# Splitting the normalised rows in the front part and re-ordering the dense part's buffers in a hybrid decoder step

## The chip, the cores and the metric

The kernel runs on one core of a Trainium2 chip. The metric is device time in microseconds (us) of the whole program, the median of several executions. One further execution was recorded by the hardware profiler; its span (first to last instruction) and its own time are given below.

## The reference

One inference step of a one-layer decoder with float32 data: a prompt of 1024 tokens (8 tiles of 128 rows) and a decode batch of 32 tokens (8 sequences of 4, called the sample tile). What matters here is the order of the computation:

```python
h = rms(x) * (1 + sc1) + sh1;  proj = h @ w_in
mix = concat(dilated_attention(proj), rwkv7(proj)) @ w_out
x = x + g1 * mix
h2 = rms(x) * (1 + sc2) + sh2            # the normalised rows of this case
x = x + g2 * peer(h2)                    # 8 heads x top-16 of 128*128 single-neuron experts
```

`peer` scores the 16384 experts by two sums of keys, takes 16 for each head, and adds `gate * gelu(h2 . u) * v` of the chosen ones.

## The kernel before

**Two ways through the experts.** For the prompt tiles 0 to 4 (`dense_set`, 640 rows) the experts are computed densely: all 16384 hidden values of a row by matmul, multiplied by a matrix of gates that is zero where an expert was not chosen, and multiplied by all of `expert_v`. For tiles 5, 6, 7 and the sample tile the 128 chosen rows of `expert_u` and `expert_v` are gathered for each token by indirect DMA.

**Precision.** A float32 matmul operand is split into two values of the type fp32r, `hi` and `lo` (`split`, line 230: a cast on ScalarE, then a subtraction on VectorE or GpSimd). `mm3` (line 243) then makes three matmuls: `hi x hi`, `hi x lo`, `lo x hi`.

**Stages in time.** Up to about 640 us: projections and part of RWKV. From 640 us to about 1690 us the *front part* (lines 1789 to 1876): RWKV of the last prompt tiles, attention, and for each tile in turn `project_out` (output projection, second norm, writes `h2A`, feature by row, two buffers), `route_scores` (scores and their best 16), `route_pick` (the 16 experts of each head) and, for tiles 0 to 4, `spread_gates` (the gate matrix, staged in a tile of 16 KB per partition and written to `g_d` in HBM). Then attention of tiles 6 and 7, `rwkv_sample` and `attn_sample`. From about 1700 us to the end the *dense part* (`dense`, line 1615) runs with the gathers and with the routing of tiles 6, 7 and the sample tile between its steps.

**How the rows reach the dense part.** In `front()` (line 1823) each dense tile's `h2A` is written to `h2_f` in HBM as float32 (line 1830, five DMAs, the last at 1248 us). At the start of the dense part (lines 1878 to 1887) `h2_f` is loaded in eight pieces into the tile `dacc`, which is free until the first output is summed there, and each piece is split into `h2T[0]` (hi) and `h2T[1]` (lo): eight casts on ScalarE and eight subtractions on VectorE, 128x640 each.

**The dense loop.** `hidden(b)` (line 1623) loads a block of `u` in two DMAs, splits it into `uh` (ScalarE) and `ul` (GpSimd), and computes for each half of the 640 rows 8 x 3 matmuls against `h2T`; GELU, gate and a split into `ch`, `cl` follow. `values` (line 1649) loads and splits `v` into `vh`, `vl`. `output` (line 1658) sums four blocks into `dacc`. Buffers: `u` three, `uh` and `ul` two each, `vh` and `vl` five each.

**What sets the order.** The parts are Python generators that `weave` (line 276) interleaves by a planner's costs; the framework then orders each engine's instructions by priority and by when their inputs and buffers are expected, and inserts the semaphores. All loads and stores go through SP's queue, in its order; the gathers go through GpSimd's. Each of SP's transfers also waits until the eighth transfer before it has landed.

**Memory.** Pools are stacks in each partition, one growing from the left and one from the right. A tile that is laid over tiles of a closed pool waits, at its first use, for the last use of every tile that it overlaps (`reuse_waits="tile"`), whichever part of it is used first. On the left lie, in bytes of a partition: `spread` 21888 to 48512 (the stage at 32128 to 48512), `tops_A` to 52608, `pick` to 63424, `front` to 88224, attention behind it. The dense pool lies over them from 22912: `dacc` to 43392, `uh` to 51584, `ul` to 59776, `u` to 65920, then `ch`, `cl`, the gates `g`, `v`, `vh`, `vl`. On the right `h2T[0]` takes 188384 to 208864 and `h2T[1]` 208864 to 229344; before them lie there the tiles of `attn_sample`, whose last one, `smo`, is at 222464 to 222976. `smo` is the attention result of the last four sample sequences; it is made from `so`, which is transposed through the one PSUM bank `rs` that `rwkv_sample`'s last transposes (of `yts`) use as well.

All engine instructions are recorded under line 196, that of a helper, so the profile's rows are told apart by the names of their tiles. `h_f` in a row is `h2_f`.

Of the kernel before, what the change touches and what calls it, by code (L numbers as in the profile page):

```python
# [11 lines left out]
FT = mybir.dt.float32  # L12
FR = mybir.dt.float32r
I32 = mybir.dt.int32
# [11 lines left out]
H = 8  # L26
# [175 lines left out]
def tile_hybrid_step(ctx, tc, ins, outs):  # L202
# [6 lines left out]
    def open_pool(es, name, side="left"):  # L209
        return es.enter_context(tc.tile_pool(name=name, bufs=1, side=side, reuse_waits="tile"))  # L210
# [1206 lines left out]
    def route_pick(pick, tops, i, eng=ve):  # L1417

        pa, place = pick
        nh = H if i < NT else 2  # L1420
        v, iu = (x[i][:, :2 * nh] for x in tops)
        eid, gate = (x[i][i][:, :TOPK * nh] for x in (eids, gates))
        fi = pa.tile([128, 16, TOPK], FT, tag="tf", name="tf", bufs=1)[:, :2 * nh]
        ve.tensor_copy(fi, iu)
        v4 = v.rearrange("p (h a) k -> p h a k", a=2)
        f4 = fi.rearrange("p (h a) k -> p h a k", a=2)
        ve.tensor_scalar(f4[:, :, 0], f4[:, :, 0], 128.0, None, op0=OP.mult)
        cand = pa.tile([128, TOPK, NCAND], FT, tag="tq", name="tc", bufs=2)[:, :nh]
        cid = pa.tile([128, H, NCAND], FT, tag="td", name="td", bufs=1)[:, :nh]
        o = 0  # L1430
        for i0, ni, nj in RECTS:
            for x, y in ((cand, v4), (cid, f4)):
                ve.tensor_tensor(x[:, :, o:o + ni * nj].rearrange("p h (i j) -> p h i j", i=ni),
                                 y[:, :, 0, i0:i0 + ni, None].to_broadcast([128, nh, ni, nj]),
                                 y[:, :, 1, None, :nj].to_broadcast([128, nh, ni, nj]), op=OP.add)
            o += ni * nj
        code = cid.bitcast(I32)
        ve.tensor_tensor(code, cid, place[:, None, :].to_broadcast([128, nh, NCAND]), op=OP.add)
        top = pa.tile([128, H, TOPK], FT, tag="tt", name="tt", bufs=1)[:, :nh]
        pu = pa.tile([128, H, TOPK], U32, tag="tp", name="tp", bufs=1)[:, :nh]  # L1440
        r = pa.tile([128, TOPK, NCAND], FT, tag="tq", name="ts", bufs=2)[:, :nh]
        for h in range(nh):
            ve.max(top[:, h, :8], cand[:, h])
        for h in range(nh):
            ve.match_replace(r[:, h], top[:, h, :8], cand[:, h], -3.0e38)
        for h in range(nh):
            ve.max_index(pu[:, h, :8], top[:, h, :8], cand[:, h])
        for h in range(nh):
            ve.max(top[:, h, 8:], r[:, h])
        for h in range(nh):  # L1450
            ve.max_index(pu[:, h, 8:], top[:, h, 8:], r[:, h])
        yield
        pf = pa.tile([128, H, TOPK], I32, tag="te", name="te", bufs=1)[:, :nh]
        ve.tensor_scalar(pf, pu.bitcast(I32), 14, None, op0=OP.logical_shift_left)
        sh = [128, TOPK, NCAND]
        eqs = []
        for h in range(nh + 1):
            if h < nh:

                eq = pa.tile(sh, I32, tag="tq", name="tq", bufs=2)  # L1460
                eqs.append(eq)
                eng.tensor_tensor(eq, code[:, h, None, :].to_broadcast(sh), pf[:, h, :, None].to_broadcast(sh), op=OP.subtract)
            if h:
                ve.tensor_reduce(eid[:, TOPK * (h - 1):TOPK * h], eqs[h - 1].bitcast(U32), axis=AX.X, op=OP.min)
                yield
        gs = pa.tile([128, H], FT, tag="th", name="th", bufs=1)[:, :nh]
        gv = gate.rearrange("p (h k) -> p h k", h=nh)
        ve.tensor_tensor(gv, top, top[:, :, :1].to_broadcast([128, nh, TOPK]), op=OP.subtract)
        sc.activation(gate, gate, AF.Exp)
        ve.tensor_reduce(gs, gv, axis=AX.X, op=OP.add)  # L1470
        ve.reciprocal(gs, gs)
        ve.tensor_tensor(gv, gv, gs[:, :, None].to_broadcast([128, nh, TOPK]), op=OP.mult)
        yield
# [138 lines left out]
        sc.copy(hi, src)  # L1612
        (gp if j in POOL_LO else ve).tensor_tensor(lo, src, hi.bitcast(FT), op=OP.subtract)

    def dense(pa, pp, acc, h2T, tiles):

        nt = len(tiles)
        n = 128 * nt
# [2 lines left out]
        gate2 = {}  # L1621

        def hidden(b):
            uh = pa.tile([128, KD, 128], FR, tag="uh", name="uh", bufs=2)
            ul = pa.tile([128, KD, 128], FR, tag="ul", name="ul", bufs=2)
            for x in range(2):
                ks = slice(4 * x, 4 * x + 4)
                u = pa.tile([128, 4, 128], FT, tag="u", name="u", bufs=3)
                sy.dma_start(u, A["uT"][b, :, ks])
                split2(u, uh[:, ks], ul[:, ks], 8 + b % 2)  # L1630
            ch = pa.tile([128, n], FR, tag="ch", name="ch", bufs=NG + EARLY)
            cl = pa.tile([128, n], FR, tag="cl", name="cl", bufs=NG + EARLY)
            for h in range(2):
                if b % 4 == 0:
                    G_[h] = pa.tile([128, n // 64, 4, 32], FT, tag="g", name="g", bufs=3)
                    sy.dma_start(G_[h], g_d[n // 64 * h:n // 64 * (h + 1), :, b:b + 4].rearrange("s e i t -> e s i t"))
                cs = slice(h * n // 2, (h + 1) * n // 2)
                ps = pp("d")
                for k in range(KD):
                    mm3(ps[:, :n // 2], (uh[:, k], ul[:, k]), [x[:, k, cs] for x in h2T], k == 0, k == KD - 1)  # L1640

                t = ps[:, :n // 2]
                sc.activation(t, t, AF.Gelu)
                tv = t.rearrange("p (s t) -> p s t", t=32)
                ve.tensor_tensor(tv, tv, G_[h][:, :, b % 4], op=OP.mult)
                split(t, ch[:, cs], cl[:, cs])
            C_[b] = (ch, cl)

        def values(grp, dh):
            for b in range(NG * grp, NG * grp + NG):  # L1650
                v = pa.tile([128, 512], FT, tag="v", name="v", bufs=2)
                sy.dma_start(v, A["expert_v"][128 * b:128 * b + 128, 512 * dh:512 * dh + 512])
                vh = pa.tile([128, 512], FR, tag="vh", name="vh", bufs=5)
                vl = pa.tile([128, 512], FR, tag="vl", name="vl", bufs=5)
                split2(v, vh, vl, b % 8)
                V_[b, dh] = (vh, vl)

        def output(grp, dh, tt):
            ps = pp("d")
            for x in range(NG):  # L1660
                b = NG * grp + x
                mm3(ps, [c[:, 128 * tt:128 * tt + 128] for c in C_[b]], V_[b, dh], x == 0, x == NG - 1)
            if grp == 0:
                ve.tensor_copy(acc[:, tt, dh], ps)
            else:
                ve.tensor_tensor(acc[:, tt, dh], acc[:, tt, dh], ps, op=OP.add)
            if grp < ngrp - 1:
                return
            i, cs = tiles[tt], slice(512 * dh, 512 * dh + 512)
            if tt == 0:  # L1670
                gate2[dh] = pa.tile([128, 512], FT, tag="act", name="g2", bufs=2)
                sy.dma_start(gate2[dh], _ap(mod_d, 5 * D + 512 * dh, [[0, 128], [1, 512]]))
            x1 = pa.tile([128, 512], FT, tag="u", name="fx", bufs=3)
            sy.dma_start(x1, x1_d[i, :, cs])
            ve.tensor_tensor(acc[:, tt, dh], acc[:, tt, dh], gate2[dh], op=OP.mult)
            ve.tensor_tensor(x1, x1, acc[:, tt, dh], op=OP.add)
            sy.dma_start(outs["y_p"][128 * i:128 * (i + 1), cs], x1)
# [106 lines left out]

    
    open_picked(ctx, "picked_5", [5])
    h2_f = dram.tile([128, KD, NDENSE], FT, name="h2_f")
    hcol = {i: 128 * i for i in dense_set}
    with ExitStack() as es:
        ps4 = open_psum(es, "frontp", at=3, sp=2)  # L1790
# [32 lines left out]
        def front():  # L1823
            for i in dense_set + [5]:
# [2 lines left out]
                    yield from until("q2")  # L1827
                yield from project_out(pf, p_fr, [i], new_x1, new_h2)
                if i in hcol:
                    sy.dma_start(h2_f[:, :, hcol[i]:hcol[i] + 128], h2A[i])  # L1830
                ready.add(("h2", i))

        def scores():
# [43 lines left out]
    open_picked(ctx, "picked", [NT, 6, 7])  # L1877
    hpd = open_pool(ctx, "h2T", "right")
    h2T = [hpd.tile([128, KD, NDENSE], FR, name=f"h2T{s}") for s in range(2)]
    pa = open_pool(ctx, "dense")  # L1880
    acc = pa.tile([128, len(dense_set), 2, 512], FT, name="dacc")
    hf = acc.rearrange("p a b c -> p (a b c)").rearrange("p (k t) -> p k t", k=KD)
    with tc.high_priority(offset=AHEAD):
        for k in range(KD):
            sy.dma_start(hf[:, k], h2_f[:, k])
        for k in range(KD):
            split(hf[:, k], h2T[0][:, k], h2T[1][:, k])
    pd = open_psum(ctx, "densep", d=4)
    all_experts = dense(pa, pd, acc, h2T, dense_set)

    def routed(pp, tiles, side):

# [107 lines left out]
```

## Time and profile before

| | us |
|---|---|
| median of 3 executions (3748.92 to 3769.43) | 3759.01 |
| the profiled execution, its own time | 3753.1 |
| its span, first to last instruction | 3751.3 |
| VectorE busy | 2693.2 (72%) |
| TensorE matmul busy | 3453.9 (92%) |
| GpSimd busy | 2080.6 (55%) |
| mean granted TensorE clock, 1 is 2.4 GHz | 0.967 |

Times in rows are us from the span's start. A row of instructions says the engine, the operation, `out<-in` by tile names, shapes, and how many were merged; in brackets the idle time of the engine before them and what ended it. Busy TensorE time overlaps for matmuls that follow each other, so it is read together with the gaps. PE is TensorE, PEld its weight loads, DVE VectorE, ACT ScalarE, POOL GpSimd, SP SyncE, SPq SP's DMA queue.

### The profile page before, as it was taken

The numbers are of one execution on the slowest core, as the hardware profiler recorded it, in microseconds if no ns is written. First come the engines' busy times: TensorE is split into PE (matmuls) and PEld (weight loads), VectorE is DVE, ScalarE is ACT, GpSimd is POOL, SyncE is SP. The second block draws the span as 40 slices with busy tenths as digits, with TensorE's granted clock in tenths as the row PEclk, the third lists the DMA queues.
The fourth block names the chain that finished last, engine by engine and source line by source line (L and its number), as shares of the span: only waits on it lengthen the run. The fifth ranks groups of instructions, "written<-read, shape, count | busy, mean of one in ns | idle before, by whom it ended". The sixth has DMA issues, their size and how long they took to land.

```text
span 3751.3 us, 57270 instructions
## 1 busy us (share of the span) xinstructions
PE 3453.9 (92%) x19618; PEld 2873.9 (77%) x19618; DVE 2693.2 (72%) x6059; ACT 1431.2 (38%) x3122; POOL 2080.6 (55%) x1842
## 2 busy tenths in 40 slices
PE   7999999789888988988999989999999999999998
PEld 3878678567767755556777778988888888898997
DVE  2556365588688656785778998787777877777787
ACT  5645345336765754543221122322223222222321
POOL 2342011015545446754655677777777777776784
PEclk8999999899999989998999999999999999999999
DMA  9653596553675568749988779999999999999997
GB/s 293 197 148 117 176 285 186 151 182 130 225 233 166 189 229 255 244 149 309 320 316 298 262 255 334 340 321 322 327 323 324 329 320 322 315 330 318 336 336 256
DMA packets 592528, 981.58 MB, mean 262 GB/s; under 512 B 78323, under 2 KB 354620, under 8 KB 589420
## 3 DMA queue, kind: packets, MB, share of 16 engines
q1 hardware_dynamic: 467788, 524.84, 43.9%
q0 software_dynamic: 124448, 453.08, 34.1%
q8 instruction: 155, 2.54, 0.3%
q14 instruction: 137, 1.12, 0.1%
HBM read 882.97 MB, written 94.78 MB: 261 GB/s over the span
## 4 chain that ended last, share of the span: by engine, by line
PE 51%; DMA 18%; DVE 14%; issue 7%; POOL 6%; ACT 3%; SPq 1%; POOLq 0%; DVEq 0%; ACTq 0%
PE d L196 23%; PE at L196 10%; PE rw L196 5%; PE pj L196 5%; DMA u<-in_uT 5%; PE rs L196 3%; POOL row L196 3%; DMA row<-in_expert_v,eid 3%; PE sp L196 2%; POOL vl L196 2%; DVE gh L196 2%; DVE ohb L196 1%; DMA v<-in_expert_v 1%; DMA w<-wq_d 1%; POOL ul L196 1%
## 5 line engine op out<-in xcount | busy, mean ns | idle before, releaser
L196 PE MATMUL d<-h2T,uh 128*128 128x320 f32 x4096 | 907.3, 311 | 18.1 <-DVE cl L196 9.0
L196 PEld LDWEIGHTS d<-h2T,uh 128*128 128x128 f32 x4096 | 689.6, 189 | 26.6 <-ACT h2T L196 8.2
L196 PE MATMUL d<-h2T,ul 128*128 128x320 f32 x2048 | 633.3, 311 | 0.6 <-POOL ul L196 0.6
L196 PE MATMUL d<-vl,ch 128*128 128x512 f32 x1280 | 508.3, 398 | 42.9 <-POOL vl L196 42.9
L196 DVE CUSTOM_DVE_ANT_0 row<-row,gh 128x1024 f32<-128x1024 f32 x416 | 500.4, 1215 | 63.5 <-DMA row<-in_expert_u,eid 50.7
L196 POOL DMA_INDIRECT row<-in_expert_u,eid x416 | 394.7, 949 | 242.0 <-DVE co L196 89.6
L196 PE MATMUL d<-vh,cl 128*128 128x512 f32 x1280 | 504.5, 395 | 0.0
L196 PE MATMUL d<-vh,ch 128*128 128x512 f32 x1280 | 478.3, 396 | 17.2 <-DVE cl L196 9.7
L196 POOL DMA_INDIRECT row<-in_expert_v,eid x416 | 397.1, 955 | 166.2 <-issue 46.2
L196 POOL TENSOR_SCALAR oha<-c_iota,tr 128x128 f32<-128x128 f32 x320 | 307.4, 966 | 312.1 <-PE sp L196 293.6
L196 POOL TENSOR_TENSOR ul<-u,uh 128x512 fp32r<-128x512 f32 x256 | 332.2, 1306 | 151.7 <-ACT uh L196 143.3
L196 ACT CAST vh<-v 128x512 fp32r<-128x512 f32 x256 | 158.8, 622 | 674.9 <-DMA v<-in_expert_v 451.9
L196 DVE SCALAR_TENSOR_TENSOR gh<-row,co,gh 128x1024 f32<-128x1024 f32 x285 | 366.1, 1285 | 48.6 <-DMA row<-in_expert_v,eid 46.7
L196 PEld LDWEIGHTS d<-h2T,ul 128*128 128x128 f32 x2048 | 386.2, 189 | 5.0 <-issue 3.7
L196 POOL TENSOR_TENSOR wl<-w,wh 128x1024 fp32r<-128x1024 f32 x50 | 123.0, 2461 | 387.2 <-ACT wh L196 326.8
L196 PEld LDWEIGHTS d<-vl,ch 128*128 128x128 f32 x1280 | 244.1, 191 | 108.0 <-POOL vl L196 58.6
L196 POOL TENSOR_TENSOR vl<-v,vh 128x512 fp32r<-128x512 f32 x224 | 289.0, 1301 | 45.7 <-ACT vh L196 42.7
L196 PEld LDWEIGHTS d<-vh,ch 128*128 128x128 f32 x1280 | 242.7, 190 | 77.5 <-DVE dacc L196 12.7
L196 ACT CAST uh<-u 128x512 fp32r<-128x512 f32 x256 | 154.8, 621 | 367.3 <-DMA u<-in_uT 212.2
L196 PEld LDWEIGHTS d<-vh,cl 128*128 128x128 f32 x1280 | 243.9, 191 | 52.8 <-issue 2.5
L196 DVE TENSOR_TENSOR dacc<-dacc,d 128x512 f32<-128x512 f32 x310 | 206.2, 683 | 47.8 <-PE d L196 47.6
L196 DVE TENSOR_TENSOR d<-d,g 128x320 f32<-128x320 f32 x256 | 126.8, 496 | 155.6 <-ACT d L196 142.4
(449 smaller groups left out, 6779.4 us busy)
## 6 DMA issues: line engine op xcount, KB each, us to landing
u<-in_uT SPq DMA_DIRECT2D x256, 256.0 KB
v<-in_expert_v SPq DMA_DIRECT2D x256, 256.0 KB
w<-wq_d SPq DMA_DIRECT2D x224, 256.0 KB
g_d<-stage SPq DMA_DIRECT2D x20, 2048.0 KB
g<-g_d SPq DMA_DIRECT2D x64, 640.0 KB
w<-in_w_in SPq DMA_DIRECT2D x75, 512.0 KB
w<-in_w_out SPq DMA_DIRECT2D x112, 256.0 KB
adaw<-in_ada_w SPq DMA_DIRECT2D x32, 512.0 KB
```

What stands on the lines that cost most here:

```text
L196: return f(*a, **k)
```

## The change

In `route_pick` two small tiles (`tf`, 1 KB per partition, and `te`, 512 B) are dropped and their results written in place. In `front()` each dense tile's `h2A` is split in four quarters, each quarter's two halves written to two HBM tensors; the dense part loads them straight into `h2T` in eight DMAs of twice the size, without cast or subtraction. The dense part's tiles are spread over three pools: `densev` (dacc, vh, vl), `denseu` (uh, ul, u), `dense` (the rest).

```diff
-        fi = pa.tile([128, 16, TOPK], FT, tag="tf", name="tf", bufs=1)[:, :2 * nh]
+        fi = iu.bitcast(FT)
         ve.tensor_copy(fi, iu)
...
-        pf = pa.tile([128, H, TOPK], I32, tag="te", name="te", bufs=1)[:, :nh]
-        ve.tensor_scalar(pf, pu.bitcast(I32), 14, None, op0=OP.logical_shift_left)
+        pf = pu.bitcast(I32)
+        ve.tensor_scalar(pf, pf, 14, None, op0=OP.logical_shift_left)
...
-    def dense(pa, pp, acc, h2T, tiles):
+    def dense(pa, pv, pu, pp, acc, h2T, tiles):
...
-            uh = pa.tile([128, KD, 128], FR, tag="uh", name="uh", bufs=2)
-            ul = pa.tile([128, KD, 128], FR, tag="ul", name="ul", bufs=2)
+            uh = pu.tile([128, KD, 128], FR, tag="uh", name="uh", bufs=2)
+            ul = pu.tile([128, KD, 128], FR, tag="ul", name="ul", bufs=2)
...
-                u = pa.tile([128, 4, 128], FT, tag="u", name="u", bufs=3)
+                u = pu.tile([128, 4, 128], FT, tag="u", name="u", bufs=3)
...
-                vh = pa.tile([128, 512], FR, tag="vh", name="vh", bufs=5)
-                vl = pa.tile([128, 512], FR, tag="vl", name="vl", bufs=5)
+                vh = pv.tile([128, 512], FR, tag="vh", name="vh", bufs=5)
+                vl = pv.tile([128, 512], FR, tag="vl", name="vl", bufs=5)
...
-    h2_f = dram.tile([128, KD, NDENSE], FT, name="h2_f")
+    h2_f = [dram.tile([128, KD, NDENSE], FT, name=f"h2_f{s}") for s in range(2)]
...
                 if i in hcol:
-                    sy.dma_start(h2_f[:, :, hcol[i]:hcol[i] + 128], h2A[i])
+                    for q in range(4):
+                        ks = slice(2 * q, 2 * q + 2)
+                        hl = [pf.tile([128, 2, 128], FR, tag=f"h2{x}", name=f"h2{x}", bufs=2) for x in "hl"]
+                        split(h2A[i][:, ks], *hl)
+                        for x in range(2):
+                            sy.dma_start(h2_f[x][:, ks, hcol[i]:hcol[i] + 128], hl[x].bitcast(FT))
...
-    pa = open_pool(ctx, "dense")
-    acc = pa.tile([128, len(dense_set), 2, 512], FT, name="dacc")
-    hf = acc.rearrange("p a b c -> p (a b c)").rearrange("p (k t) -> p k t", k=KD)
+
+    pv, pu, pa = (open_pool(ctx, x) for x in ("densev", "denseu", "dense"))
+    acc = pv.tile([128, len(dense_set), 2, 512], FT, name="dacc")
     with tc.high_priority(offset=AHEAD):
-        for k in range(KD):
-            sy.dma_start(hf[:, k], h2_f[:, k])
-        for k in range(KD):
-            split(hf[:, k], h2T[0][:, k], h2T[1][:, k])
+        for k in range(0, KD, 2):
+            for x in range(2):
+                sy.dma_start(h2T[x].bitcast(FT)[:, k:k + 2], h2_f[x][:, k:k + 2])
```

By the sizes of the tiles, the pick pool then ends at 61888 and the front pool lies from there to 90784; in the dense part `dacc`, `vh` and `vl` take 22912 to 63872, `uh`, `ul` and `u` 63872 to 86400, and the rest 86400 to 135552. `h2T` stays where it was.

## Rows read from the trace of the kernel before

**Rows 1.** The page: span, and the chain that ended last by engine.
```profile
span 3751.3 us, 57270 instructions
...
PE 51%; DMA 18%; DVE 14%; issue 7%; POOL 6%; ACT 3%; SPq 1%; POOLq 0%; DVEq 0%; ACTq 0%
```

**Rows 2.** Stretches: start:end, length, busy us (x instructions) by engine, TensorE clock, DMA share, GB/s.
```profile
700.00:1250.00 550.00, 473.68 (x2779) 388.72 (x2778) 425.57 (x1631) 327.27 (x802) 225.67 (x213) 0.95 0.59 187
1640.00:1690.00 50.00, 33.81 (x212) 24.04 (x210) 48.52 (x159) 20.07 (x46) 28.63 (x18) 0.83 0.23 87
1690.00:1704.00 14.00, 0.95 (x6) 0.55 (x6) 3.41 (x15) 5.55 (x12) 1.41 (x2) 0.66 0.93 300
1704.00:1712.00 8.00, 6.83 (x26) 6.44 (x27) 6.86 (x10) 5.88 (x10) 4.21 (x2) 0.53 1.07 305
1712.00:1728.00 16.00, 14.04 (x96) 13.78 (x94) 4.67 (x9) 5.67 (x11) 8.41 (x8) 1.00 1.02 326
1728.00:1800.00 72.00, 71.36 (x333) 53.27 (x334) 43.96 (x82) 15.09 (x29) 43.01 (x40) 0.98 0.93 317
```

**Rows 3.** PE in order of time, 1690 to 1707 us.
```profile
1693.78 0.43 PE L196 MATMUL rs<-c_ident,yts 32*128 32x32 f32 x4 [4.61 <-DVE yts L196]
1695.55 0.47 PE L196 MATMUL rs<-c_ident,so 128*128 128x128 f32 x1 [1.34 <-ACT gno L196]
1703.95 0.90 PE L196 MATMUL d<-h2T,uh 128*128 128x320 f32 x2 [7.93 <-ACT h2T L196]
1706.02 0.64 PE L196 MATMUL d<-h2T,uh 128*128 128x320 f32 x1 [1.17 <-DVE h2T L196]
```

**Rows 4.** DVE in order of time, 1632 to 1711 us.
```profile
1632.60 4.64 DVE L196 TENSOR_TENSOR ohb<-c_iota,tr 128x256 f32<-128x256 f32 x1
...
1643.47 1.00 DVE L196 TENSOR_REDUCE so<-som 128x128 f32<-128x512 f32 x1
...
1696.36 0.43 DVE L196 TENSOR_TENSOR smo<-soT 128x16 f32<-128x16 f32 x4 [0.21 <-ACT soT L196]
1705.14 5.97 DVE L196 TENSOR_TENSOR h2T<-dacc,h2T 128x640 fp32r<-128x640 f32 x8 [8.35 <-DMA mix_d<-smo]
```

**Rows 5.** SP's queue in order of time, 1690 to 1699 us.
```profile
1690.71 3.71 SPq L196 DMA_DIRECT2D dacc<-h_f  x8
1694.52 1.14 SPq L196 DMA_DIRECT2D u<-in_uT  x2
1697.73 1.61 SPq L196 DMA_DIRECT2D mix_d<-smo  x1
```

**Rows 6.** The chain that ended last, 1684 to 1707 us: start, length, what.
```profile
1684.99 1.64 DMA yts<-ys_d
...
1692.09 5.58 DMA dacc<-h_f
1697.73 7.29 DMA mix_d<-smo
```

**Rows 7.** Groups of ACT and DVE instructions: xcount, busy us, mean ns, idle before.
```profile
L196 ACT CAST hT<-h 128x256 fp32r<-128x256 f32 x8 | 3.0, 403 | 2.7 <-DMA h<-hT_d 2.7
...
L196 DVE TENSOR_TENSOR hT<-h,hT 128x256 fp32r<-128x256 f32 x8 | 3.1, 420 | 1.1 <-ACT hT L196 1.1
...
L196 DVE TENSOR_TENSOR ohb<-c_iota,tr 128x256 f32<-128x256 f32 x190 | 91.4, 494 | 17.7 <-PE sp L196 16.7 <-ACT tr L196 0.6
```

**Rows 8.** Transfers that read or write h2_f: issue ns, first and last start.
```profile
L196 SPq DMA_DIRECT2D dacc<-h_f x8: 398/430/430, 1690.7 to 1694.0; - x8
L196 SPq DMA_DIRECT2D h_f<-h2A x5: 529/538/565, 718.8 to 1247.9; - x5
```

**Rows 9.** POOL in order of time at 1632 us, and two of its groups.
```profile
1632.44 4.52 POOL L196 TENSOR_TENSOR st<-st,t 128x2048 f32<-128x2048 f32 x1
...
L196 POOL TENSOR_SCALAR oha<-c_iota,tr 128x128 f32<-128x128 f32 x191 | 183.7, 968 | 180.5 <-PE sp L196 168.7 <-ACT kT L196 4.4 <-ACT oha L196 4.3
...
L196 POOL TENSOR_TENSOR ul<-u,uh 128x512 fp32r<-128x512 f32 x256 | 332.2, 1306 | 151.7 <-ACT uh L196 143.3
```

More of the change, by code (lines that the diff above doesn't have):

```diff
@@ L1672, in output @@
                 sy.dma_start(gate2[dh], _ap(mod_d, 5 * D + 512 * dh, [[0, 128], [1, 512]]))
-            x1 = pa.tile([128, 512], FT, tag="u", name="fx", bufs=3)
+            x1 = pu.tile([128, 512], FT, tag="u", name="fx", bufs=3)
             sy.dma_start(x1, x1_d[i, :, cs])
@@ L1879, in tile_hybrid_step @@
     h2T = [hpd.tile([128, KD, NDENSE], FR, name=f"h2T{s}") for s in range(2)]
-    pa = open_pool(ctx, "dense")
-    acc = pa.tile([128, len(dense_set), 2, 512], FT, name="dacc")
-    hf = acc.rearrange("p a b c -> p (a b c)").rearrange("p (k t) -> p k t", k=KD)
+    pv, pu, pa = (open_pool(ctx, x) for x in ("densev", "denseu", "dense"))
+    acc = pv.tile([128, len(dense_set), 2, 512], FT, name="dacc")
     with tc.high_priority(offset=AHEAD):
-        for k in range(KD):
-            sy.dma_start(hf[:, k], h2_f[:, k])
-        for k in range(KD):
-            split(hf[:, k], h2T[0][:, k], h2T[1][:, k])
+        for k in range(0, KD, 2):
+            for x in range(2):
+                sy.dma_start(h2T[x].bitcast(FT)[:, k:k + 2], h2_f[x][:, k:k + 2])
     pd = open_psum(ctx, "densep", d=4)
-    all_experts = dense(pa, pd, acc, h2T, dense_set)
+    all_experts = dense(pa, pv, pu, pd, acc, h2T, dense_set)
     def routed(pp, tiles, side):
```

## The prediction

> **What bounds the kernel now.** I read the page's chain of work that ended last first: TensorE holds 51% of it, DMA 18%, VectorE 14%, ScalarE 3%, SP's queue 1% [rows 1]. The change acts in two places, so the next view is busy time by stretch [rows 2]. From 700 to 1250 us, where the dense tiles' rows are made, PE is busy for 473.7 of 550 us, DVE for 425.6, ACT for 327.3, POOL for 225.7, the DMA engines for 59%. From 1640 to 1690 us, the front's last attention, DVE is the full one (48.5 of 50 us) and PE has 33.8. From 1690 to 1704 us PE has 0.95 of 14 us: this is the hole the change aims at. Afterwards PE is nearly gapless (71.4 of 72 us from 1728 to 1800), so what the hole costs is not recovered from slack behind it, and a shift of its end shifts the program's end.
>
> What ends the hole? The order of PE's instructions shows the last transposes of the front (`yts`, then `so`) at 1693.8 and 1695.6, one pair of dense matmuls at 1703.95, and the steady stream from 1706.02, after an idle time ended by DVE's `h2T` [rows 3]. DVE's first `h2T` subtraction sat idle for 8.35 us, and not for `dacc`: what came last was the DMA that stores `smo` [rows 4]. `h2T[1]` lies over `smo`, so its first write waits until that store has landed. The chain agrees: a `dacc` load to 1697.67, then the `smo` store for 7.29 us [rows 6]; SP issued that store at 1697.73, the moment the load had landed, although `smo` was finished at 1696.8 [rows 4, 5]. This store stays in the changed kernel, and so does the place of `h2T[1]`.
>
> **The change, part by part.** The profiled execution took 3753.1 us, 5.9 less than the median of 3759.0; I sum against it and carry the difference over to the median.
>
> *In-place results in `route_pick`.* The same instructions with another output address: nothing. The two small tiles they replace only shrink the pool. The tile in place of `te` is held until GpSimd has read it, but `te` was itself held that long, so no new wait arises.
>
> *Splits in the front: 5 tiles x 4 quarters.* 20 casts of 128x256 at 0.403 us are 8.1 us of ACT; 20 subtractions at 0.420 us are 8.4 us of DVE, or 9.9 at the 0.494 us that `ohb`, of the same size and made beside POOL's work, takes [rows 7]. Bounds: nothing, if all lie beside PE; 18.0 us, if all lie on the path. ACT and DVE hold 3% and 14% of the chain, so I take 8.1 x 0.03 + 9.9 x 0.14 = 1.6 us.
>
> *Transfers in the front.* 40 writes take the place of 5. An issue costs between 0.398 and 0.538 us [rows 8], so SP gains between 40 x 0.398 - 5 x 0.538 = 13 and 19 us of issuing in 550. Behind a write that waits for its subtraction stand the weight loads of the scores and the output projection. The bytes grow by 2.62 MB; at 187 GB/s for a 59% share [rows 2], or 317 GB/s at full use, that is 8.3 us of DMA. By the chain's shares, 19 x 0.01 + 8.3 x 0.18 = 1.7 us; bounds 0 and 27.
>
> *The dense buffers.* `uh`, `ul` and `u` then lie over the front pool, free once tile 5's scores are made, and no longer over the stage and the picks. So the first four pieces of `u` can be loaded and split before 1690. PE has nothing to gain from that as long as `h2T` is late. It moves four `ul` subtractions of 1.306 us [rows 9] into the stretch in which DVE is full. There the trace shows what POOL's two-input work does: while POOL's `st` ran for 4.52 us, DVE's `ohb` took 4.64 instead of 0.42 [rows 4, 7, 9]. Bounds: nothing, if they fall beside DVE work that isn't held, and 4 x 1.306 = 5.2 us, if DVE stands for each; I take half, 2.6 us, because RWKV's last steps, which end in `yts` and `so`, are DVE work in that stretch. Casts of `u` on ACT are covered there (20 of 50 us busy).
>
> The Trainium skill, "SBUF — State Buffer", section "SBUF: two separate sides", says that GpSimd and a VectorE instruction with two SBUF inputs exclude each other for a whole instruction; the 4.64 us agrees, and by that rule this term would be the full 5.2 us. That is 2.6 us more than I take.
>
> *The loads and the start.* Gone are eight casts and subtractions and eight `dacc` loads. `h2T[0]` lies over tiles read for the last time before 1640, so its four loads can go early, into a DMA system that is 23% used [rows 2]. The four loads of `h2T[1]` must wait for `smo`; behind them on SP stand the gates, `v` and the store of RWKV's sample rows. The store of `smo` can now be issued at about 1696.9, with no `dacc` load ahead of it. Its landing is unknown: between the 1.64 us of the small `yts` load and the 7.29 us it took behind 2.6 MB [rows 6]; some gates and `v` will be ahead, so I take the middle, 4.5 us, hence 1701.4. A load of 0.655 MB then takes 0.4 us to issue, 1.6 us as for `yts`, and 2.1 us for its bytes at 305 to 326 GB/s [rows 2]: the first lands at 1705.5, the fourth at 1711.8, with 1.6 us of matmuls left (six at 0.263 us, as 26 take 6.83 us before 1712, at a granted clock of 0.53, near the 1.2 GHz level). So the first half block ends near 1713.4. Before, it ended at about 1711.9: 26 matmuls had begun by 1712 [rows 2], and one half block is 24. That is +1.5 us. Bounds: -13 us, if the hole (14.0 - 0.95) closes, and +5.2 us, if the store lands as late as before (first load at 1709.2, last at 1715.5, end at 1717.1).
>
> **Sum:** 1.6 + 1.7 + 2.6 + 1.5 = 7.4 us: 3753.1 becomes 3760.5 and the median 3766.
>
> **The rivals.**
>
> *The hole closes.* If the order of the front's last steps changes so that `smo` is stored before the attention ends, all of `h2T` is there by 1690 and dense matmuls also fill PE's idle time before it. Price: 13 us of the hole and at most 50 - 33.8 = 16.2 us before it, so 3730 to 3746. For it: `so` was ready at 1644.5 and only waited for its transpose until 1695.6, behind `yts` [rows 3, 4]. Against it: both go through one PSUM bank in the planned order, which the change has no reason to turn round, and DVE, which a dense block needs too, is full. Chance 0.22, of which 0.15 is faster by over 0.5%. A measurement of this kernel can tell about 0.5%, 18.8 us, from no change: the three executions spread over 0.55%.
>
> *The front stalls on its two-deep ring (slower).* The third and fourth quarter reuse the buffers of the first and second, so ACT's cast, in ACT's order, waits until four small stores have landed. Price: one such wait for each of 5 tiles at 1.64 to 7.29 us [rows 6], so 8 to 36 us. It decides from 3.8 us of landing (5 x 3.8 = 19). For it: DMA is 59% used there, and RWKV's chain passes ACT. Against it: ACT is idle for 40% of the stretch. Time 3774 to 3802; chance 0.15, 0.13 of it slower by over 0.5%.
>
> *Every new subtraction waits for POOL.* In the front POOL's `oha` takes 0.968 us [rows 9]. If each of the 20 stood for a whole one, that is 19.4 us: 3785. The trace speaks against it: `ohb`, with POOL busy for 41% of the stretch, has a mean of only 0.494 against 0.420 us undisturbed [rows 2, 7]. The rule cited above would have it so wherever both meet. Chance 0.05, slower.
>
> *It doesn't do what it says.* The store of `smo` lands as late as before, behind gates and `v`: +5.2 in place of +1.5, 3770. Chance 0.12, within 0.5%.
>
> **How the numbers follow.** The forecast has 0.46. Faster: 0.15. Slower: 0.13 + 0.05 = 0.18. Within 0.5%: 0.46 + 0.12 + 0.07 + 0.02 = 0.67. The range reaches down to 3736, into the closed hole, and up to 3794, into the stalled front; about 0.08 lies beyond each end.
>
> **What would show it.** Right: PE's hole still begins near 1690 and the stream of dense matmuls is steady from about 1712; the idle time before `d<-h2T` is ended by the loads of `h2T`, whose second tensor is issued after the `smo` store; `u` is loaded before 1690. Wrong on the good side: dense matmuls before 1695. Wrong on the slow side: ACT's casts of `h2A` idle for the stores, and the front's end later by over 15 us. If the front's end moves by more than 15 us either way without these signs, the order of the front changed, which no term here holds.

## The result and the profile after

The changed kernel is slower: its median is 3814.02 us (3804.74 to 3821.23), beside 3761.57 us for the kernel before on the same chip; the ratio is 1.0141 [1.0104, 1.0178]. That is 52 us, and it lies outside the range given above. The profiled execution took 3821.23 us, 68 us more than that of the kernel before; the rows below come from these two executions, which differ by more than the medians do.

The page of the changed kernel, the span and the chain of waits by engine, against [rows 1]:

```profile
span 3819.4 us, 57444 instructions
...
PE 48%; DMA 19%; DVE 15%; POOL 8%; issue 7%; ACT 3%; SPq 1%; POOLq 0%; DVEq 0%; ACTq 0%
```

TensorE's share of the chain falls and GpSimd's rises. The page doesn't say where. Two long stretches do, from 640 to 1800 us and from there to 3735 us, first of the kernel before, then of the changed one (columns as in [rows 2]):

```profile
640.00:1800.00 1160.00, 1001.05 (x5677) 753.54 (x5677) 821.39 (x2713) 609.00 (x1454) 540.13 (x457) 0.93 0.64 206
1800.00:3735.00 1935.00, 1865.23 (x10140) 1644.59 (x10139) 1536.54 (x2598) 518.08 (x1034) 1382.91 (x1280) 0.99 0.91 316
```

```profile
1690.00:1745.00 55.00, 14.27 (x24) 1.83 (x22) 17.64 (x18) 5.19 (x8) 28.69 (x10) 0.58 0.43 140
1745.00:1757.00 12.00, 1.08 (x5) 0.68 (x5) 1.02 (x7) 2.73 (x6) 1.87 (x2) 0.50 0.57 169
1757.00:1765.00 8.00, 6.07 (x26) 5.67 (x27) 0.00 (x0) 0.00 (x0) 0.00 (x0) 0.59 1.02 411
1765.00:1781.00 16.00, 14.98 (x100) 14.45 (x100) 3.48 (x8) 4.75 (x12) 3.78 (x3) 1.00 0.93 298
640.00:1800.00 1160.00, 956.62 (x5459) 720.55 (x5458) 776.65 (x2667) 604.02 (x1451) 515.83 (x433) 0.91 0.61 198
1800.00:3735.00 1935.00, 1854.42 (x10021) 1628.41 (x10021) 1515.85 (x2596) 512.40 (x1024) 1374.25 (x1274) 0.98 0.91 315
```

Up to 1800 us PE does 44.4 us less work (1001.05 - 956.62), in the later stretch only 10.8 us less, which no run here explains. So most of the loss is made ahead of the dense part. The first four rows show its shape: from 1690 to 1745 us PE is busy for 14 of 55 us, and the stream of dense matmuls that before was full from 1712 is full from 1765. PE in order of time in the changed kernel, against [rows 3]:

```profile
1706.70 1.91 PE L196 MATMUL rs<-vs,spT 32*32 32x512 f32 x2
1745.09 0.60 PE L196 MATMUL rs<-c_ident,yts 32*128 32x32 f32 x4 [36.48 <-DVE yts L196]
1747.03 0.48 PE L196 MATMUL rs<-c_ident,so 128*128 128x128 f32 x1 [1.33 <-ACT gno L196]
1757.68 1.43 PE L196 MATMUL d<-h2T,uh 128*128 128x320 f32 x4 [10.18 <-DMA h2T<-h_f]
```

PE stood idle for 36.48 us until `yts`, the output of `rwkv_sample`, was there; before, that wait was 4.61 us. The front's other work on PE was finished by then. Three markers tell it, in the kernel before and then in the changed one: the updates of RWKV's state `S` for the prompt (first and last start), the stores of `smo` on SP, and the attention's `om`:

```profile
L196 DVE SCALAR_TENSOR_TENSOR S<-rw,PC,c_mask_bd x40: 296/344/356, 655.4 to 1281.2; 128x128 f32<-128x128 f32 x40
L196 SPq DMA_DIRECT2D mix_d<-smo x2: 371/991/1611, 1521.4 to 1697.7; - x2
L196 DVE TENSOR_TENSOR om<-om,at x16: 269/284/293, 1033.9 to 1690.0; 128x128 f32<-128x128 f32 x16
```

```profile
L196 DVE SCALAR_TENSOR_TENSOR S<-rw,PC,c_mask_bd x40: 341/344/352, 656.7 to 1340.6; 128x128 f32<-128x128 f32 x40
L196 SPq DMA_DIRECT2D mix_d<-smo x2: 371/379/387, 1602.9 to 1748.3; - x2
L196 DVE TENSOR_TENSOR om<-om,at x16: 270/280/316, 1034.7 to 1682.8; 128x128 f32<-128x128 f32 x16
```

At 656 us both kernels stand alike. The prompt's last `S` is then 59.4 us late, the last `smo` 50.6 us, while the last `om` is 7.2 us *early*. The front's two halves have traded places: the independent work (attention, scores, gates) runs ahead, the serial chain of RWKV falls behind, and the front ends with the later of the two.

Where does the chain lose? The prompt has 40 updates of `S`, in five groups of eight. They start 1.3, 7.8, 27.4, 55.7 and 58.5 us later than before: nearly all is lost between the second group and the fourth. From the second to the third the engine to look at is PE (the bounds are the starts of the two groups, before and then after; columns as in [rows 2]):

```profile
856.40:930.30 73.90, 71.34 (x498) 57.81 (x499) 63.65 (x251) 50.76 (x128) 43.71 (x42) 1.00 0.37 118
864.20:957.70 93.50, 86.43 (x583) 71.79 (x582) 71.95 (x262) 64.54 (x163) 54.45 (x52) 0.96 0.45 147
L196 PE MATMUL at<-w,m 128*128 128x256 f32 x50 | 12.1, 380 | 0.0
```

The stretch is 19.6 us longer, and PE works for 15.1 us more in it. The third line, from the stretch after, is work of the other half: 50 matmuls of an output projection, of which the kernel before has none there.

From the third group to the fourth it is DVE. One of the chain's stages there is a triangular solve on DVE, 31 pairs of a product `ttmp` and a sum into `tv`, each waiting for the one before. Between the load of its input and the transfer of its result lie 70 us before (1052 to 1122) and 93 us after (1091 to 1184). DVE's groups in these two stretches, before:

```profile
L196 DVE TENSOR_TENSOR ttmp<-tv,mu__11005 128x2 f32<-128x2 f32 (+30 forms) x31 | 14.9, 480 | 0.3
L196 DVE TENSOR_TENSOR ohb<-c_iota,tr 128x256 f32<-128x256 f32 x33 | 14.4, 455 | 0.9 <-PE sp L196 0.9
L196 DVE TENSOR_REDUCE tv<-ttmp 128x1 f32<-128x2 f32 (+30 forms) x31 | 10.5, 340 | 0.5
L196 DVE MAX8 tv<-at 128x8 f32<-128x128 f32 x16 | 4.1, 290 | 0.0
```

and after:

```profile
L196 DVE TENSOR_TENSOR ohb<-c_iota,tr 128x256 f32<-128x256 f32 x37 | 19.1, 533 | 1.8 <-PE sp L196 1.7
L196 DVE TENSOR_TENSOR ttmp<-tv,mu__11092 128x2 f32<-128x2 f32 (+30 forms) x31 | 17.1, 553 | 0.3
L196 DVE TENSOR_REDUCE tv<-ttmp 128x1 f32<-128x2 f32 (+30 forms) x31 | 10.3, 333 | 0.2
L196 DVE TENSOR_REDUCE eid<-tq 128x16 int32<-128x800 uint32 x8 | 7.8, 972 | 0.0
L196 DVE MAX8 tv<-at 128x8 f32<-128x128 f32 x20 | 5.0, 293 | 2.3 <-PE at L196 2.3
```

The solve itself grew by 2.0 us (14.9 + 10.5 to 17.1 + 10.3). The rest of the 23 us is routing that DVE was given between its pairs: 20 scores in place of 16, 37 `ohb` in place of 33, eight `eid`. DVE hardly idles in either (5 and 4 us). It is the other half's work that goes first, because the instructions stand so in its order.

### The profile page after: what moved, and what is told of

It reads as the page before. It is cut to its first block, busy times and chain, and to the rows that moved or that the text cites. A ratio compares the mean times of both kernels' runs of the same rounds, so it can differ in the third digit from the quotient of the medians.

```text
span 3819.4 us, 57444 instructions
## 1 busy us (share of the span) xinstructions
PE 3460.9 (91%) x19618; PEld 2879.9 (75%) x19618; DVE 2685.1 (70%) x6071; ACT 1432.9 (38%) x3134; POOL 2080.4 (54%) x1842
## 4 chain that ended last, share of the span: by engine, by line
PE 48%; DMA 19%; DVE 15%; POOL 8%; issue 7%; ACT 3%; SPq 1%; POOLq 0%; DVEq 0%; ACTq 0%
PE d L196 20%; PE at L196 10%; DMA u<-in_uT 6%; PE rw L196 5%; PE pj L196 5%; POOL row L196 3%; DMA row<-in_expert_v,eid 3%; PE sp L196 3%; PE rs L196 2%; DVE gh L196 2%; POOL vl L196 2%; DMA v<-in_expert_v 1%; POOL ul L196 1%; DVE ttmp L196 1%; DVE tv L196 1%
## 5 line engine op out<-in xcount | busy, mean ns | idle before, releaser
L196 POOL TENSOR_TENSOR vl<-v,vh 128x512 fp32r<-128x512 f32 x224 | 288.0, 1296 | 75.7 <-ACT vh L196 70.6
L196 PE MATMUL sp<-oha,ohb 128*128 128x128 f32 x1280 | 212.5, 299 | 37.6 <-DVE ohb L196 16.3
L196 PEld LDWEIGHTS sp<-oha,ohb 128*128 128x128 f32 x1280 | 189.9, 207 | 75.1 <-issue 21.7
```

The source lines that it names most:

```text
L196: return f(*a, **k)
```

## The experiments

Theories, as the expectations name them: A, the split changes the order, and RWKV's chain falls behind. B, the 40 writes hold SP's queue. C, the new places of the buffers make something wait. D, split and transfers cost what they cost wherever they stand. E, the loads of `h2T` that wait for `smo` are the loss. The markers of every run, from its profile (start in us of the prompt's last `S`, the last store of `smo`, the last `om`; PE's busy time from 640 to 1800). They are of the profiled execution, whose own time is not always near the median: 3782 us in e4, 3796 in e9, 3783 in e10.

| kernel | median | ratio to before, 95% | S | smo | om | PE |
|---|---|---|---|---|---|---|
| before | 3759 to 3764 | 1 | 1281.2 | 1697.7 | 1690.0 | 1001 |
| changed | 3814.02 | 1.0141 [1.0104, 1.0178] | 1340.6 | 1748.3 | 1682.8 | 957 |
| e1 no split | 3749.31 | 0.9972 [0.9957, 0.9987] | 1282.3 | 1700.0 | 1693.7 | 1007 |
| e2 split alone | 3809.16 | 1.0137 [1.0099, 1.0175] | 1337 | 1739 | 1670 | 959 |
| e3 casts, subtractions only | 3771.34 | 1.0030 [1.0015, 1.0045] | 1336.2 | 1718.6 | 1651.1 | 977 |
| e4 writes only | 3794.81 | 1.0103 [1.0067, 1.0139] | 1271.8 | 1699.7 | 1718.6 | 978 |
| e5 split behind the scores | 3756.93 | 0.9992 [0.9977, 1.0007] | 1294 | 1699 | 1691 | 993 |
| e6 halves | 3770.54 | 1.0028 [1.0009, 1.0046] | 1296 | 1714 | 1711 | 998 |
| e7 subtractions on GpSimd | 3746.09 | 0.9968 [0.9950, 0.9987] | 1285.8 | 1668.5 | 1660.7 | 993 |
| e8 writes on ScalarE's queue | 3776.51 | 1.0045 [1.0028, 1.0061] | 1291 | 1691 | 1728 | 971 |
| e9 planner not charged | 3781.16 | 1.0047 [1.0031, 1.0063] | 1271.3 | 1693.4 | 1722.7 | 985 |
| e10 planner charged, no split | 3777.82 | 1.0031 [1.0012, 1.0050] | 1298.7 | 1731.8 | 1691.7 | 965 |
| e11 behind the scores, on GpSimd | 3749.72 | 0.9959 [0.9945, 0.9974] | 1287.0 | 1697.8 | 1695.3 | 1003 |
| e12 h2T clear of smo | 3805.12 | 1.0135 [1.0099, 1.0171] | 1337 | 1736.5 | 1671 | 964 |
| e13 as e11, clear of smo | 3751.38 | 0.9979 [0.9961, 0.9997] | 1285 | 1695 | 1693 | 1003 |

Over these 15 profiled executions the span grows by 0.92 us for each us by which the later of `smo` and `om` moves (correlation 0.91), and single ones lie up to 16 us off that line. So the front's end tells most of the time, and not all of it: e3 and e4 end their fronts together (1718.6) and differ by 0.7% in their medians.

**Which part of the change?** First everything but the split (e1: `h2_f` in float32, loaded through `dacc`, but with the in-place tiles and three dense pools), then the split with the one dense pool of before (e2; its buffers fit only with the in-place tiles).

```diff
 e1, against the changed kernel
-                    for q in range(4): ... split ... two writes
+                    sy.dma_start(h2_f[:, :, hcol[i]:hcol[i] + 128], h2A[i])
```

> The changed kernel without the split in the front: rows go to HBM as float32 and are loaded through dacc as before; the in-place tiles and the three dense pools stay. Theory A (the casts and subtractions of the split, put among the front's work, let the front's attention and scores pass RWKV's chain in the engines' order, and smo is late): the time of the kernel before, 3750 to 3770, first dense matmul at 1700 to 1712. Theory B (the 40 writes on SP's queue hold RWKV's loads up): the same, 3750 to 3770. Theory C (the new places of buffers make something wait): 3800 to 3825, first dense matmul near 1757.

> The kernel before with the split in the front, the direct loads and the in-place tiles (the room for the split's buffers comes from these), but with the one dense pool of before. Theories A and B: 3800 to 3825, first dense matmul at 1745 to 1765, the state S updated for the last time near 1328. Theory C: 3750 to 3775, first dense matmul at 1700 to 1715.

e1 is 0.28% faster than before, e2 is as slow as the change. C falls: the whole loss comes with the split. In passing, e1 shows what the hole ahead of the dense part can be. PE in order of time:

```profile
1698.75 0.47 PE L196 MATMUL rs<-c_ident,so 128*128 128x128 f32 x1 [1.34 <-ACT gno L196]
1700.20 1.43 PE L196 MATMUL d<-h2T,uh 128*128 128x320 f32 x4 [0.98 <-ACT h2T L196]
1702.81 0.64 PE L196 MATMUL d<-h2T,uh 128*128 128x320 f32 x1 [1.17 <-DVE h2T L196]
```

`dacc` is loaded before `smo` is stored, so only casts and subtractions stay behind it, and PE idles for 2 us in place of 9. (It idles again, for 4.4 us, ahead of the next tiles' output projection at 1719 us, so not all of this is kept.)

**Which part of the split?** The casts and subtractions without their writes, results unused (e3); the writes without casts and subtractions, to two further tensors that nothing reads (e4; the five float32 writes stay, so it stores 2.6 MB more than the change does).

```diff
 e3, against the kernel before with the in-place tiles
                     sy.dma_start(h2_f[:, :, hcol[i]:hcol[i] + 128], h2A[i])
+                    for q in range(4): ... split(h2A[i][:, ks], *hl)
 e4, against the kernel before
                     sy.dma_start(h2_f[:, :, hcol[i]:hcol[i] + 128], h2A[i])
+                    for q in range(4):
+                        for x in range(2):
+                            sy.dma_start(h2_x[x][:, ks, hcol[i]:hcol[i] + 128], h2A[i][:, ks])
```

> The kernel before with the in-place tiles and with the 20 casts and 20 subtractions in the front, whose results are not stored or used; the rows still go as float32 in 5 writes. Theory A: slower by 40 to 80 us, 3800 to 3840, S for the last time later than 1310. Theory B: 3750 to 3772, S for the last time near 1270. Theory C: 3750 to 3772.

> The kernel before with 40 more writes in the front (each quarter of h2A twice, as float32, into two HBM tensors that nothing reads), no casts or subtractions. Theory A: 3745 to 3772. Theory B: 3795 to 3825, S for the last time later than 1310. Theory C: 3750 to 3772.

Half a hit each. e3 makes `S` as late as the change does (1336.2), as A said, but its sample part ends 30 us sooner than in the changed kernel, and the time is 0.3% up, not the 1% that A gave at least. e4 is 1.0% slower, at the lower edge of what B gave, yet not B's way: `S` is early (1271.8), and it is the attention that ends late (`om` at 1718.6), after which PE waits for the next tiles' rows. The two parts push the order opposite ways, and each costs. Their costs add up to that of the split (0.3 and 1.0 to 1.4%), which D would have too; the next runs speak against D.

**The same instructions at another place.** e5 keeps every cast, subtraction and write and issues them behind the tile's scores. e6 splits in halves, with one buffer of each kind in place of two. e7 gives the subtractions to GpSimd. e8 issues the writes from ScalarE's queue.

```diff
 e5, against the changed kernel: the block moves from front() into scores()
                 yield from route_scores(pf, p_fr, {i: h2A[i]}, tops)
+                if i in hcol: ... the split and its eight writes
 e6
-                    for q in range(4):
+                    for q in range(2): ... tiles [128, 4, 128], bufs=1 ...
 e7
-                        split(h2A[i][:, ks], *hl)
+                        split(h2A[i][:, ks], *hl, eng=gp)
 e8
-                            sy.dma_start(h2_f[x][:, ks, hcol[i]:hcol[i] + 128], hl[x].bitcast(FT))
+                            sc.dma_start(h2_f[x][:, ks, hcol[i]:hcol[i] + 128], hl[x].bitcast(FT))
```

> The changed kernel with the same casts, subtractions and 40 writes of a tile issued in the program behind the tile's scores, not ahead of them. Theory A (the loss is the order: the front's work passes RWKV's chain on DVE): the chain's last S update back at 1270 to 1300, first dense matmul at 1695 to 1725, 3745 to 3785. Theory D (the split's work and its transfers cost what they cost, wherever in the front they stand): S near 1335, first dense matmul at 1740 or later, 3800 to 3825.

> The changed kernel with each tile split in two halves, not four quarters: 10 casts, 10 subtractions, 20 writes, the same bytes and the same buffer space (one buffer of each kind). Theory A: the order is dealt anew; which way can't be said from the number of instructions, but the first dense matmul follows the end of RWKV's sample part: S near 1270 to 1300 gives 3750 to 3785, S near 1335 gives 3800 to 3825. Theory D: half of the issuing gone, the bytes kept: between 3785 and 3805, S between 1300 and 1325.

> The changed kernel with the 20 subtractions of the split on GpSimd, not on VectorE. If the subtractions on DVE delay RWKV's chain by standing in its way: S back at 1270 to 1300 and 3745 to 3785. Theory D with the writes as its main cost: S near 1335, 3800 to 3825.

> The changed kernel with the 40 writes issued by ScalarE on its own DMA queue, not by SP. Theory B (SP's queue, in order, holds what stands behind a write that waits): 3745 to 3775, S at 1270 to 1300, first dense matmul at 1695 to 1715. Theory D (bytes and split work): unchanged, 3800 to 3825. Theory A: the order is dealt anew, 3745 to 3825, and the first dense matmul goes with the end of RWKV's sample part and of the attention, whichever is later.

D falls with e5: the same 80 instructions and the same bytes, and the loss is gone (0.9992 against 1.0141). e7 is faster than before, with the same bytes and writes. In all four `S` is back at 1286 to 1296 us, and the time follows the later of `smo` and `om`, but for e7, which ends its front 29 us sooner than before and gains only 0.3%. Its PE waits elsewhere:

```profile
PE at L196 <- DMA w<-in_w_out: 26.1, 1, 26.1
```

There the next tiles' output projection stands ahead of the dense matmuls in PE's order, and its weights queue behind `h2T`. e8 has the same wait. The hole has moved, not gone. (e8 alone would fit B but for 1.5 us; B fell with e4, where 40 writes on SP's queue leave RWKV early.)

**Work or sequence?** The order is made in two steps: `weave` deals out the steps of the parts by a planner's costs, then the framework orders each engine's instructions. e9 runs the changed kernel, but its planner isn't told of the split's casts and subtractions (it still counts the writes, which in its arithmetic move no step), so it deals the front's steps out as before; e10 has no split, but its planner is charged for one and deals as in the changed kernel.

```diff
 e9, against the changed kernel
-                        split(h2A[i][:, ks], *hl)
+                        nc.scalar.copy(hl[0], h2A[i][:, ks])
+                        nc.vector.tensor_tensor(hl[1], h2A[i][:, ks], hl[0].bitcast(FT), op=OP.subtract)
 e10, against e1
+                        meter.add("sc", "copy", hs, hs)
+                        meter.add("ve", "tensor_tensor", hs, hs)
+                        for x in range(2):
+                            meter.add("sy", "dma_start", hs, hs)
```

> The changed kernel, every instruction of it, but the planner that interleaves the parts is not told the cost of the 20 casts and 20 subtractions, so that it deals out the front's steps in the sequence of the kernel before. Theory A (order): S for the last time at 1260 to 1300, first dense matmul at 1690 to 1725, 3740 to 3785. Theory D (the split's instructions and transfers cost what they cost): S near 1335, 3800 to 3825.

> No split in the front (float32 rows, five writes, as in the run without the split), but the planner is charged for the 20 casts, 20 subtractions and 40 writes, so that it deals out the front's steps in the sequence of the changed kernel. If that sequence alone makes RWKV late: S for the last time at 1320 to 1345, 3795 to 3825. If it takes the split's instructions as well (sequence and instructions together move the order on DVE): S at 1270 to 1300, 3745 to 3775. Theory D: 3745 to 3765.

e10 does the work of e1 and no more (in both PE has 19618 instructions, DVE 6059, GpSimd 1842) and is 0.6% slower (1.0031 to 0.9972): a different sequence alone puts `smo` 32 us later. Its 3778 us lies between its two cases, nearer the second: the sequence alone does part of it. e9 has the instructions of the changed kernel and is 0.9% faster (1.0047 to 1.0141), as A said, if only just (3781 of at most 3785). Its markers, and then those of e10:

```profile
L196 DVE SCALAR_TENSOR_TENSOR S<-rw,PC,c_mask_bd x40: 330/343/351, 660.3 to 1271.3; 128x128 f32<-128x128 f32 x40
L196 SPq DMA_DIRECT2D mix_d<-smo x2: 370/1082/1794, 1480.3 to 1693.4; - x2
L196 DVE TENSOR_TENSOR om<-om,at x16: 262/276/289, 1057.8 to 1722.7; 128x128 f32<-128x128 f32 x16
```

```profile
L196 DVE SCALAR_TENSOR_TENSOR S<-rw,PC,c_mask_bd x40: 327/343/353, 657.6 to 1298.7; 128x128 f32<-128x128 f32 x40
L196 SPq DMA_DIRECT2D mix_d<-smo x2: 359/368/377, 1556.1 to 1731.8; - x2
L196 DVE TENSOR_TENSOR om<-om,at x16: 263/277/289, 1034.1 to 1691.7; 128x128 f32<-128x128 f32 x16
```

In e9 RWKV is early and the attention late, in e10 the reverse. Against e1, sequence alone costs 0.6%, the instructions alone 0.75%, both together 1.7%: the sum and a little more, within the intervals.

**Two repairs, and the wait on `smo`.** e11 joins e5 and e7. e12 and e13 lay the last small tiles of the sample attention at the low end of their pool, so that `smo` no longer lies under `h2T`.

```diff
 e12, against the changed kernel (e13: against e11), at the start of attn_sample
+            for tag, shape in (("hmr", [128, H]), ("so2", [128, 128]), ("soT", [128, 4, H, 4]), ("smo", [128, 4, 4, 4])):
+                pa.tile(shape, FT, tag=tag, name=tag, bufs=2)
```

> Two repairs together: the split issued behind the tile's scores, and its subtractions on GpSimd. Theory A: S at 1270 to 1295; if the two gains over the changed kernel (57 and 68 us) have one cause they don't add up: 3735 to 3765. If they had two causes that add up: below 3715.

> The changed kernel with the last small tiles of the sample attention (smo among them) laid at the low end of their pool, so that nothing of h2T lies over them and its loads need not wait for the store of smo. Theory A (the front's end, set by RWKV's late sample part, is the loss): smo still near 1748, the 24th dense matmul at 1750 to 1756 in place of 1764.8, 3795 to 3812. Theory E (the wait of the loads of h2T on smo is the loss): 3755 to 3775, dense matmuls from before 1715.

> The kernel with the split behind the scores and its subtractions on GpSimd, and with the same move of the sample attention's last tiles. Theory A: the front ends as in that kernel without the move (smo near 1698), and the gap between smo and the dense matmuls closes: 24th dense matmul at 1700 to 1706, 3732 to 3748. If the gap doesn't limit: 3745 to 3755.

e11's two repairs don't add up, so they mend one thing; at 0.9959 it beats both kernels, as do e1 and e7, and the intervals don't tell these three apart. e12 gives A's time (3805), with a front that ended 12 us sooner in its profile, and e13's gap didn't close (14.45 us idle ahead of the first dense matmul); its time, 3751, is that of its other case, but the gap that it was to close was still there. Neither shows the wait itself, for the loads stayed where they were. SP in order of time in e12:

```profile
1736.54 0.39 SPq L196 DMA_DIRECT2D mix_d<-smo  x1
1736.97 0.49 SPq L196 DMA_DIRECT2D g<-mod_d  x1
1737.56 3.77 SPq L196 DMA_DIRECT2D h2T<-h_f  x6
```

All of `h2T`, the half that never lay over `smo` included, stands behind the store in SP's order. That E isn't the loss follows all the same from the hole's size, below; what the wait on `smo` is worth for the direct loads stays open.

## Why the prediction was wrong

**The step that failed** is the sum over the front. It read the split as 20 casts and 20 subtractions in a fixed order, weighted by each engine's share of the chain (1.6 us), and the writes likewise (1.7 us). Their own price was indeed small. In the changed kernel the subtractions, and who waited in all for the split's `h2h`:

```profile
L196 DVE TENSOR_TENSOR h2l<-h2A,h2h x20: 376/422/1322, 720.6 to 1267.0; 128x256 fp32r<-128x256 f32 x20
...
  ACT h2h L196: 5.5, 3
  DVE h2l L196: 4.3, 3
```

But e10 loses 0.6% without any of this work, and e5 loses nothing with all of it. The term missing was which instruction goes first on the engines that both halves of the front use, PE and DVE; its price is how much later the later half ends, 50.6 us here (`smo` stored at 1748.3 and not 1697.7). The prediction's last sentence named the case ("the order of the front changed, which no term here holds") and gave it neither a chance nor a price; the sentence that the change "has no reason to turn round" the planned order was an assumption. The two transposes did keep their order; the halves of the front did not.

**The in-place tiles and the dense buffers**: nothing and a loss of 2.6 us were forecast. e1 has both and is 12 us faster than the kernel before by its median (0.28% by the ratio), with `dacc` loaded five microseconds sooner and the hole down to 2 us. The sign was wrong. The early splits of the dense part did enter RWKV's sample chain, as feared, but not by DVE standing for GpSimd's work. DVE and then GpSimd in order of time in the changed kernel:

```profile
1689.45 2.29 DVE L196 TENSOR_TENSOR t<-st,vec 128x2048 f32<-128x2048 f32 x1
1699.91 0.69 DVE L196 TENSOR_TENSOR vl<-v,vh 128x512 fp32r<-128x512 f32 x1 [8.16 <-ACT vh L196]
1700.52 2.28 DVE L196 TENSOR_REDUCE sa<-t 128x32 f32<-128x2048 f32 x1
1701.51 1.27 POOL L196 TENSOR_TENSOR vl<-v,vh 128x512 fp32r<-128x512 f32 x1 [17.54 <-ACT vh L196]
1702.73 4.50 POOL L196 TENSOR_TENSOR st<-st,vec 128x2048 f32<-128x2048 f32 x1
1710.77 2.48 POOL L196 TENSOR_TENSOR vl<-v,vh 128x512 fp32r<-128x512 f32 x2
```

The chain's `t` was done at 1691.74. Its next steps, `sa` on DVE and `st` on GpSimd, each stood behind a `vl` that waited for `vh`, whose cast waited until a load of `v` had landed (16.47 us idle on ScalarE, to 1699.26). For `st` that is 11.0 us (1702.73 - 1691.74), and the two `vl` at 1710.77 add 2.5 us at most: up to 13.5 of the 50 us, an estimate from these rows. e12 has the same wait (8.44 us on DVE). It isn't a price of the new pools alone: in e2, with the one pool of before, three `ul` and a `vl` run on GpSimd directly ahead of the same step (1677.5 to 1691.9). It is the same story once more: what belongs to another part goes first.

**The start of the dense part** (+1.5 us) came out right in size, and by luck. From the transpose of `so` to the 26th dense matmul it took 1712.0 - 1695.55 = 16.4 us before [rows 2, 3] and 1765.0 - 1747.03 = 18.0 us after, +1.6. So E can't hold the loss. But the forecast had four loads of `h2T` go early, and none did. The fair comparison is with e1, which needs 1707.6 - 1698.75 = 8.9 us for its 26: the direct loads lengthen a hole that is short without them (e1's later 4.4 us of idle time set against it).

**The rivals.** The front's two-deep ring cost 4.9 us in two waits of ScalarE, not 8 to 36. Subtractions that stand for GpSimd's work: their median stayed at 0.422 us. The longest took 1.322 us, and it ran beside a GpSimd product of two tiles:

```profile
797.01 2.92 POOL L196 TENSOR_TENSOR moF<-mab,c_mask_o 128x512 f32<-128x512 f32 x2 [163.17 <-DVE rr L196]
797.46 1.32 DVE L196 TENSOR_TENSOR h2l<-h2A,h2h 128x256 fp32r<-128x256 f32 x1
```

The rule cited from the Trainium skill, "SBUF — State Buffer", section "SBUF: two separate sides", fits that one. It didn't hold beside `oha`, which the rival was about: the six subtractions that began while an `oha` was running took 0.376 to 0.429 us. On GpSimd (e7) the subtractions took 0.726 us each in the median. The closed hole came nearest in e1, without the direct loads. The slow end of the forecast, 3794 us, was too low because no rival had the front's halves trading places.

What stays open is why the framework prefers one instruction to another at the single place; the runs show only that a small edit turns it, and which way the front's end then goes.

## What to carry to other kernels

Where a planner and a list scheduler make the order, an edit's price is not its instructions times their share: look first at the parts that run side by side, which of them ends last, and how far they are apart, for any edit can move that by tens of microseconds. Measure one edit that costs nothing (another sequence of the same instructions: 0.6% here) before believing a gain or loss of that size. And try the same edit at another place in the program before giving it up: the split was worth -1.4% ahead of the scores and nothing behind them.

## What was not expected

Nearly every order has a hole at the end of the front. PE's longest idle time there is 8 us before and 4 us in e1, and 13 to 49 us in all the others, not always with the same wait at its end: `yts` in the changed kernel, e2, e3, e10 and e12, the loads of `h2T` in e5, e6, e11 and e13, the next tiles' rows in e4, the weights of their output projection in e7, e8 and e9. While PE waits, its granted clock is down: 0.58 from 1690 to 1745 us and 0.59 in the first 8 us of dense matmuls, near the 1.2 GHz level, and 1.00, the 2.4 GHz level, from 1765. Before, it was 0.66 in the hole, 0.53 in the 8 us behind it, then 1.00 [rows 2]. So the hole also slows the 26 matmuls behind it.
